# One-hot operands of a gate-matrix product: pairs of tokens interleaved, eight tokens written by each VectorE instruction

## The chip, the cores and the metric

The kernel runs on one core of a Trainium2 chip. The metric is the device time of one execution in microseconds (us). The kernel before took a median of 3380.77 us over three runs (3378.14 to 3381.57).

## The reference

The whole program is two transformer-like blocks over 512 tokens of 1024 features. The change lies in the last part of the second block, a feed-forward layer that gathers single-neuron experts by product keys:

```python
def peer_ffn(xn, w_q, sub_keys, u, v):
    def block(xb):
        q = (xb @ w_q).reshape(PEER_BLOCK, PEER_HEADS, 2, PEER_HALF)
        s = jnp.einsum('thpd,hpnd->thpn', q, sub_keys).astype(jnp.float32)
        s_top, i_top = lax.top_k(s, PEER_TOPK)
        cand = s_top[:, :, 0, :, None] + s_top[:, :, 1, None, :]
        cand_idx = i_top[:, :, 0, :, None] * PEER_N_KEYS + i_top[:, :, 1, None, :]
        ...
        best, pos = lax.top_k(cand, PEER_TOPK)
        expert = jnp.take_along_axis(cand_idx, pos, axis=-1)
        g = jax.nn.softmax(best, axis=-1)
        act = jax.nn.gelu(jnp.einsum('td,thkd->thk', xb, u[expert]), approximate=False)
        return jnp.einsum('thk,thkd->td', (g * act).astype(xb.dtype), v[expert])
```

There are 8 heads, 128 keys on each of the two sides, so 128 x 128 = 16384 experts, and each head of each token takes 16 of them. A token thus has 128 picks: two key numbers (k1 and k2) and a weight g for each.

## The kernel before, in words

**Dense experts.** For the last 128 tokens the kernel gathers the picked rows of u and v by indirect DMA. For the first 384 tokens (three tiles of 128, NDENSE is 3) it computes all 16384 experts: for each of 128 pieces of 128 experts, hidden = gelu(u piece x tokens) (u_task), then hidden times gates (weigh), then the product with the v piece (v_task, L1755). The gates are zero for experts that a token did not pick.

**The gate matrix.** For each token gate_matrix(i) makes the 128 x 128 matrix of gates G[k2, k1] as a product over the token's 128 picks: a one-hot of k2 (picks on the partitions, 128 keys along the row) as weights, and the weighted one-hot of k1 as the moving operand. Both are fp16; the weight is split into two fp16 parts, so a token takes two matmuls that add up in PSUM (L1443). `picks[i]` holds, per pick (partition) and token, k1, k2 and the two parts of the weight; `it16` holds the 128 key numbers in each partition. The steps of gate_matrix, four tokens at a time, are

- `rows` and `fill` (L1430 to L1437): three tiles for eight tokens each, of ten such tiles in all (tag "t", NT = 10). VectorE writes them with three narrow instructions of 128 elements per token: the one-hot of k2 (L1433), and for each part of the weight the one-hot of k1 times the part, in one instruction with two operations (L1436). The picks of the token are its per-partition scalars.
- `product` (L1443), two steps (eight tokens) later: eight matmuls of four tokens into one PSUM tile. PSUM has four such tiles in this phase, which the expert products of u_task use too.
- `store` (L1452, L1456), three steps (twelve tokens) later: ScalarE moves the PSUM tile in two halves to staging tiles; every sixteen tokens these go to DRAM (`gate_d`). `load_gates` (L1684) brings the gates of eight pieces back, and `weigh` (L1728) multiplies them into the hidden values.

```python
for t0 in range(0, 128 + 12, 4):
    if t0 - 12 in ps:
        store(t0 - 12, ps.pop(t0 - 12))
    ...
    if 0 <= t0 - 8 < 128:
        ps[t0 - 8] = product(t0 - 8, oh[(t0 - 8) // 8 * 8])
    yield
```

**The order of the work.** gate_matrix is a generator in a list of background work (`W.later`), one for each of the three token tiles, behind top-k steps of VectorE (`top_k`, L1314 to L1390) that find the picks. It runs between the first 28 products of u_task, which read the weights directly in fp32: 8 matmul instructions of 384 columns per piece at L1708, two records each in the trace, 16 records per piece. After each piece the pace of this stage (PACE[6] = 6.5) lets six or seven background steps follow. What is left over after the 28 pieces is run at once (`W.flush`), then the gates are loaded and the v products begin (L1755). Each engine works through its instructions in program order, in the order in which a scheduler has put them; VectorE's and ScalarE's order in this stage also holds the splitting of v pieces into two parts (L151 on VectorE, L143 on ScalarE, into tiles "hi" and "lo").

Other lines named below: L1378 is a VectorE comparison of top-k, 1024 fp16 elements, with an operand that is broadcast; L973 subtracts from each block of a cumulated sum one of its elements, repeated; L498 is a fp32 product of the first block with 128 columns; L883 is a projection of the second block; L1720 is the Gelu behind L1708.

Of the kernel before, what the change touches and what calls it, by code (L numbers as in the profile page):

```python
# [9 lines left out]
F16 = mybir.dt.float16  # L10
# [3 lines left out]
OP = mybir.AluOpType  # L14
# [155 lines left out]
def tile_kernel(ctx: ExitStack, tc: tile.TileContext, ins, out):  # L170
    nc = tc.nc
# [14 lines left out]
    def ps_tile(role="a"):  # L186
        tag, n = psum["roles"].get(role, psum["roles"]["a"])
        return psum["pool"].tile([128, 512], F32, tag=tag, bufs=n, name="ps")
# [101 lines left out]
    sm = ctx.enter_context(tc.tile_pool(name="sm", bufs=2))  # L290
    hp = ctx.enter_context(tc.tile_pool(name="hold", bufs=1))
    blocks = ExitStack()
    g = blocks.enter_context(tc.tile_pool(name="g", bufs=1, reuse_waits="tile"))
    NT = 10
# [5 lines left out]
    def tb(name, n=T + 2):  # L300
        return sm.tile([128, n], F32, tag="t", bufs=NT, name=name)
# [521 lines left out]
    it128 = hp.tile([128, 128], F32, name="it128")  # L823
# [2 lines left out]
    glp = hp.tile([128, 2, KD, 16], F32R, name="glp")  # L826
    idx = {NDENSE: hp.tile([128, NSLOT], I32, name="idx")}
    gw = {NDENSE: hp.tile([128, NSLOT], F32, name="gw")}
    it16 = hp.tile([128, 128], F16, name="it16")
    it1 = hp.tile([128, TOPK], F16, name="it1")  # L830
    picks = {i: hp.tile([128, 4, 128], F16, name=f"picks{i}") for i in range(NDENSE)}
    dram = ctx.enter_context(tc.tile_pool(name="dram", bufs=1, space=bass.MemoryType.DRAM))
# [4 lines left out]
    def second_block():  # L837
# [3 lines left out]
            def tables():  # L841
                for t, name in ((cols2, "cols2"), (it128, "it128"), (reset, "reset"), (wup, "wup")):
                    nc.sync.dma_start(t, ins[name])
                nc.vector.tensor_copy(it1, it128[:, :TOPK])
                nc.vector.tensor_copy(it16, it128)
                w = tb("glw", KD * 16).rearrange("p (k c) -> p k c", c=16)
                nc.sync.dma_start(w, ins["glw"])
                split_act([glp[:, 0], glp[:, 1]], w)
                for i in range(2):
                    m = g.tile([128, T], F32, tag="table", bufs=2, name="masks")[:, :512]  # L850
                    m = m.rearrange("p (a b) -> p a b", b=128)
                    nc.sync.dma_start(m, ins["masks"][:, 4 * i:4 * i + 4])
                    masks.extend(m[:, j] for j in range(4))

                l0, l1 = cols2[:, E_LG:E_LG + 4], cols2[:, E_LG + 4:E_LG + 8]
                mx, e0, e1 = (sm.tile([128, 4], F32, name=n) for n in ("mx", "e0", "e1"))
                nc.vector.tensor_tensor(out=mx, in0=l0, in1=l1, op=OP.max)
                nc.vector.tensor_tensor(out=e0, in0=l0, in1=mx, op=OP.subtract)
                nc.vector.tensor_tensor(out=e1, in0=l1, in1=mx, op=OP.subtract)
                nc.scalar.activation(e0, e0, AF.Exp)  # L860
                nc.scalar.activation(e1, e1, AF.Exp)
                nc.vector.tensor_tensor(out=e1, in0=e0, in1=e1, op=OP.add)
                nc.vector.reciprocal(out=e1, in_=e1)
                nc.vector.tensor_tensor(out=lb, in0=e0, in1=e1, op=OP.mult)
                nc.vector.tensor_scalar(out=omlb, in0=lb, scalar1=-1.0, scalar2=1.0, op0=OP.mult, op1=OP.add)
# [555 lines left out]
            def gate_matrix(i):  # L1421

                k1, k2, *w = (picks[i][:, j] for j in range(4))
                stage = []

                def rows(t0):

                    oh = [sm.tile([128, 8, 128], F16, tag="t", bufs=NT, name="oh") for _ in range(3)]
                    return oh

                def fill(t0, oh):
                    for t in range(t0, t0 + 4):
                        nc.vector.tensor_scalar(out=oh[0][:, t % 8], in0=it16, scalar1=k2[:, t:t + 1],  # L1433
                                                scalar2=None, op0=OP.is_equal)
                        for x, y in zip(oh[1:], w):
                            nc.vector.tensor_scalar(out=x[:, t % 8], in0=it16, scalar1=k1[:, t:t + 1],  # L1436
                                                    scalar2=y[:, t:t + 1], op0=OP.is_equal, op1=OP.mult)  # L1437

                def product(t0, oh):
                    ps = ps_tile("g").rearrange("p (t n) -> p t n", n=128)  # L1440
                    for t in range(4):
                        for j in (1, 2):
                            nc.tensor.matmul(ps[:, t], oh[0][:, t0 % 8 + t], oh[j][:, t0 % 8 + t],  # L1443
                                             start=j == 1, stop=j == 2)
                    return ps

# [8 lines left out]
                        if t0 % 16 == 12:  # L1455
                            nc.scalar.dma_start(gate_d[:, (128 * i + t0) // 16, j * 1024:(j + 1) * 1024], stage[j])  # L1456

                oh, ps = {}, {}
                for t0 in range(0, 128 + 12, 4):
                    if t0 - 12 in ps:  # L1460
                        store(t0 - 12, ps.pop(t0 - 12))
                    if t0 < 128:
                        if t0 % 8 == 0:
                            oh[t0] = rows(t0)
                        fill(t0, oh[t0 // 8 * 8])
                    if 0 <= t0 - 8 < 128:
                        ps[t0 - 8] = product(t0 - 8, oh[(t0 - 8) // 8 * 8])
                    yield
# [73 lines left out]
            for word in PLAN.split():  # L1542
# [4 lines left out]
                else:  # L1547
                    name = word.rstrip("01234")
# [402 lines left out]
```

## Time and profile before

| what | value |
|---|---|
| median of three runs | 3380.77 us (3378.14 to 3381.57) |
| profiled execution, its own time | 3379.18 us |
| span of the profiled execution | 3377.2 us |
| mean granted TensorE clock | 0.985 |
| TensorE busy | 98% of the span |
| VectorE busy | 64% |
| ScalarE busy | 39% |
| GpSimd busy | 5% |

The profile is one execution. Its span runs from the first to the last instruction; 1.98 us of the execution's time lie around it. The page cuts the span into 40 slices of 84.4 us; a digit is the busy share in tenths, and the row PEclk is the clock that TensorE was granted. Records whose operands have shape 128x384 or 128x512 with "f32" are fp32 products, those with "f16" the gate products.

### The profile page before, as it was taken

The page shows a single profiled execution, that of the slowest core. Times are in us where ns is not written, and L with a number is a line of the kernel's source. Part 1 is how long each engine was busy: PE and PEld are TensorE (multiplying, and loading weights), DVE is VectorE, ACT ScalarE, POOL GpSimd, SP SyncE. Part 2 cuts the span into 40 slices and gives each one's busy share as a digit, 9 for nine tenths or more (in the row PEclk, how much of TensorE's full clock was granted, in tenths as well). Part 3 has the DMA queues.
Part 4 walks back from the last instruction along what each step waited for, and adds up shares of the span by engine and source line. Part 5 has one row for each costly group of instructions (what it writes and reads, how often), then busy time and mean ns, then how long its engine had stood idle before and what let it go on. Part 6 is the DMA issues. An engine that isn't in the chain of part 4 may idle for free.

```text
span 3377.2 us, 52075 instructions
## 1 busy us (share of the span) xinstructions
PE 3313.5 (98%) x21063; PEld 2989.4 (89%) x21063; DVE 2152.3 (64%) x4979; ACT 1302.9 (39%) x2388; POOL 184.7 (5%) x132
## 2 busy tenths in 40 slices
PE   8999999999999999999999999898899999999999
PEld 7999999999899999999999988554589999999998
DVE  6545554334654555433566679999988888888544
ACT  5433333324433333332554543444433333333333
POOL 0000000000000000000000000000032222222000
PEclk9999999999999999999999999988999999999999
DMA  5222222223422222222422133334599998999542
GB/s 210 85 85 85 76 76 88 92 97 113 159 85 73 97 83 87 88 100 88 150 76 88 63 124 139 134 141 149 197 351 351 340 347 320 342 346 344 189 150 94
DMA packets 129968, 532.10 MB, mean 158 GB/s; under 512 B 9136, under 2 KB 60992, under 8 KB 73280
## 3 DMA queue, kind: packets, MB, share of 16 engines
q1 hardware_dynamic: 103520, 368.19, 30.6%
q0 software_dynamic: 18432, 134.23, 10.3%
q10 hardware_dynamic: 7776, 26.37, 2.0%
q8 instruction: 165, 2.70, 0.3%
q14 instruction: 75, 0.61, 0.1%
HBM read 501.48 MB, written 27.26 MB: 157 GB/s over the span
## 4 chain that ended last, share of the span: by engine, by line
PE 84%; DVE 12%; DMA 2%; ACT 1%; issue 1%; POOL 0%; DVEq 0%; ACTq 0%; POOLq 0%
PE ps L386 36%; PE ps L1755 13%; PE ps L1711 12%; PE ps L454 5%; DVE oh L1436 5%; PE ps L887 3%; DVE oh L1433 2%; PE ps L549 2%; PE ps L688 2%; PE ps L1004 2%; PE ps L1275 1%; PE ps L396 1%; PE ps L498 1%; PE ps L883 1%; PE ps L450 1%; DMA uv<-uv,idx 1%
## 5 line engine op out<-in xcount | busy, mean ns | idle before, releaser
L151 DVE TENSOR_TENSOR lo<-raw,hi 128x1024 fp32r<-128x1024 f32 x532 | 650.3, 1223 | 745.5 <-ACT hi L143 742.9
L143 ACT ACTIVATE hi<-raw 128x1024 fp32r<-128x1024 f32 x532 | 563.0, 1059 | 1390.4 <-PE ps L386 626.9
L386 PE MATMUL ps<-xnh,hi 128*128 128x256 f32 (+1 forms) x2464 | 513.7, 283 | 0.0
L386 PE MATMUL ps<-xnl,hi 128*128 128x256 f32 (+1 forms) x2464 | 513.5, 283 | 0.0
L386 PE MATMUL ps<-xnh,lo 128*128 128x256 f32 (+1 forms) x2464 | 512.8, 283 | 0.0
L1755 PE MATMUL ps<-hi,hw 128*128 128x512 f32 x1536 | 428.9, 395 | 10.3 <-DVE hw L204 9.3
L1711 PE MATMUL ps<-hn,hi 128*128 128x384 f32 x1600 | 408.4, 336 | 0.0
L386 PEld LDWEIGHTS ps<-xnh,lo 128*128 128x128 f32 x2464 | 385.8, 189 | 0.0
L386 PEld LDWEIGHTS ps<-xnh,hi 128*128 128x128 f32 x2464 | 384.7, 188 | 1.1
L386 PEld LDWEIGHTS ps<-xnl,hi 128*128 128x128 f32 x2464 | 384.4, 188 | 0.1
L1755 PEld LDWEIGHTS ps<-hi,hw 128*128 128x128 f32 x1536 | 288.2, 189 | 72.8 <-DVE hw L204 12.0
L1625 POOL DMA_INDIRECT uv<-uv,idx x128 | 184.5, 1441 | 2946.4 <-DVE hw L204 2450.5
L1711 PEld LDWEIGHTS ps<-hn,hi 128*128 128x128 f32 x1600 | 290.4, 188 | 4.3
L1711 PE MATMUL ps<-hn,lo 128*128 128x384 f32 x800 | 268.6, 336 | 0.0
L1755 PE MATMUL ps<-lo,hw 128*128 128x512 f32 x768 | 239.9, 392 | 0.0
L1436 DVE TENSOR_SCALAR oh<-it,picks 128x128 f16<-128x128 f16 x768 | 204.9, 313 | 0.0
L1708 PE MATMUL ps<-hn,raw 128*128 128x384 f32 x448 | 172.0, 545 | 1.8 <-ACT stage L1452 1.0
L1755 PEld LDWEIGHTS ps<-lo,hw 128*128 128x128 f32 x768 | 144.9, 189 | 32.0
L1653 DVE SCALAR_TENSOR_TENSOR acc<-uv,dots,acc 128x1024 f32<-128x1024 f32 x127 | 163.0, 1283 | 3.2
L1661 DVE SCALAR_TENSOR_TENSOR uv<-uv,hnT 128x1024 f32<-128x1024 f32 x128 | 155.7, 1218 | 10.8 <-DMA uv<-uv,idx 10.8
L1708 PEld LDWEIGHTS ps<-hn,raw 128*128 128x128 f32 x448 | 94.1, 215 | 67.1 <-issue 20.9
L1711 PEld LDWEIGHTS ps<-hn,lo 128*128 128x128 f32 x800 | 150.0, 188 | 0.1
(354 smaller groups left out, 5257.5 us busy)
## 6 DMA issues: line engine op xcount, KB each, us to landing
raw<-ws SPq DMA_DIRECT2D x313, 1024.0 KB, 4.8
gate_d<-stage ACTq DMA_DIRECT2D x48, 512.0 KB, 3.5
gates<-gate_d SPq DMA_DIRECT2D x16, 1536.0 KB, 9.7
dm<-decay_m SPq DMA_DIRECT2D x8, 264.0 KB, 5.7
vb<-vbias SPq DMA_DIRECT2D x8, 256.0 KB, 5.5
dc<-decay SPq DMA_DIRECT2D x8, 256.0 KB, 5.6
uv<-uv,idx POOLq DMA_INDIRECT x128, 8.3
h<-ht SPq DMA_DIRECT2D x2, 544.0 KB, 5.6
```

What stands on the lines that cost most here:

```text
L143: nc.scalar.activation(hi, raw[i], AF.Copy)
L151: nc.vector.tensor_tensor(out=lo, in0=r, in1=parts[i][0].bitcast(F32), op=OP.subtract)
L386: nc.tensor.matmul(t[:, :b - a], w[wi][:, off + k, :], x[k].t[xi][:, a:b], start=(k == 0 and n == 0), stop=(k == K - 1 and n == 2))
L454: nc.tensor.matmul(p, xn[k].t[xi][:, m0:m0 + mn], w[wi][:, kk, :], start=(k == 0 and n == 0), stop=(k == KD - 1 and n == 2))
L887: nc.tensor.matmul(p, parts[wi][:, k, :], x[k][:, xi], start=(k == 0 and n == 0), stop=(k == K - 1 and n == 2))
L1436: nc.vector.tensor_scalar(out=x[:, t % 8], in0=it16, scalar1=k1[:, t:t + 1], scalar2=y[:, t:t + 1], op0=OP.is_equal, op1=OP.mult)
L1625: nc.gpsimd.indirect_dma_start(out=t, out_offset=None, in_=ins["uv"], in_offset=bass.IndirectOffsetOnAxis(ap=idx[i][:, j:j + 1], axis=0))
L1653: nc.vector.scalar_tensor_tensor(out=acc, in0=v, scalar=dots[:, j:j + 1], in1=acc, op0=OP.mult, op1=OP.add)
L1661: nc.vector.scalar_tensor_tensor(out=u, in0=u, scalar=1.0, in1=hnT, op0=OP.mult, op1=OP.mult, accum_out=dots[:, j:j + 1])
L1708: nc.tensor.matmul(ps, w[0][:, k, :], tl["hn32"][k][:, :ND], start=k == 0, stop=k == KD - 1)
L1711: nc.tensor.matmul(ps, w[wi][:, k, :], tl["hn"][k][:, xi], start=(k == 0 and n == 0), stop=(k == KD - 1 and n == 2))
L1755: mm = nc.tensor.matmul(tl["acc"][t][b], h[:, hi, t * 128:(t + 1) * 128], w[vi][:, b * 512:(b + 1) * 512], start=(e == 0 and n == 0), stop ...
```

## The change

`it16` now holds each key number twice, side by side. A one-hot tile is still 128 x 1024 fp16 and still for eight tokens, but its layout is [4 pairs of tokens, 128 keys, 2 tokens of the pair]. For eight tokens VectorE writes two tiles with one instruction each, the bare one-hots of k1 and k2 (L1438 of the changed kernel, `rows`): the first operand is the key table, read again for each pair, the second are the picks of eight tokens, of which a pair is read again for each of the 128 keys. One step of four tokens later `weighed` multiplies the one-hot of k1 by each part of the weight into two more tiles (L1445). So a group of eight tokens takes four tiles instead of three, of the same ten, and 192 wide instructions take the place of 1152 narrow ones. The matmuls (now L1453) read a token's operands with a step of two elements. `store` is the same; lines behind gate_matrix move by 10 (L1452 to L1462, L1708 to L1718, L1720 to L1730, L1728 to L1738, L1755 to L1765).

```diff
--- before.py
+++ after.py
@@ -826,7 +826,7 @@
     glp = hp.tile([128, 2, KD, 16], F32R, name="glp")
     idx = {NDENSE: hp.tile([128, NSLOT], I32, name="idx")}
     gw = {NDENSE: hp.tile([128, NSLOT], F32, name="gw")}
-    it16 = hp.tile([128, 128], F16, name="it16")
+    it16 = hp.tile([128, 128, 2], F16, name="it16")
     it1 = hp.tile([128, TOPK], F16, name="it1")
     picks = {i: hp.tile([128, 4, 128], F16, name=f"picks{i}") for i in range(NDENSE)}
     dram = ctx.enter_context(tc.tile_pool(name="dram", bufs=1, space=bass.MemoryType.DRAM))
@@ -842,7 +842,7 @@
                 for t, name in ((cols2, "cols2"), (it128, "it128"), (reset, "reset"), (wup, "wup")):
                     nc.sync.dma_start(t, ins[name])
                 nc.vector.tensor_copy(it1, it128[:, :TOPK])
-                nc.vector.tensor_copy(it16, it128)
+                nc.vector.tensor_copy(it16, it128[:, :, None].to_broadcast([128, 128, 2]))
                 w = tb("glw", KD * 16).rearrange("p (k c) -> p k c", c=16)
                 nc.sync.dma_start(w, ins["glw"])
                 split_act([glp[:, 0], glp[:, 1]], w)
@@ -1421,26 +1421,36 @@
             def gate_matrix(i):
 
                 k1, k2, *w = (picks[i][:, j] for j in range(4))
+                full = [128, 4, 128, 2]
+                keys = it16[:, None].to_broadcast(full)
                 stage = []
 
+                def wide(x, t0):
+                    return x[:, t0:t0 + 8].rearrange("p (a b) -> p a b", b=2)[:, :, None, :].to_broadcast(full)
+
+                def row():
+                    return sm.tile([128, 4, 128, 2], F16, tag="t", bufs=NT, name="oh")
+
                 def rows(t0):
 
-                    oh = [sm.tile([128, 8, 128], F16, tag="t", bufs=NT, name="oh") for _ in range(3)]
+                    oh = [row() for _ in range(2)]
+                    for x, k in zip(oh, (k1, k2)):
+                        nc.vector.tensor_tensor(out=x, in0=keys, in1=wide(k, t0), op=OP.is_equal)
                     return oh
 
-                def fill(t0, oh):
-                    for t in range(t0, t0 + 4):
-                        nc.vector.tensor_scalar(out=oh[0][:, t % 8], in0=it16, scalar1=k2[:, t:t + 1],
-                                                scalar2=None, op0=OP.is_equal)
-                        for x, y in zip(oh[1:], w):
-                            nc.vector.tensor_scalar(out=x[:, t % 8], in0=it16, scalar1=k1[:, t:t + 1],
-                                                    scalar2=y[:, t:t + 1], op0=OP.is_equal, op1=OP.mult)
+                def weighed(t0, oh):
+
+                    parts = [row() for _ in w]
+                    for x, y in zip(parts, w):
+                        nc.vector.tensor_tensor(out=x, in0=oh[0], in1=wide(y, t0), op=OP.mult)
+                    return [oh[1], *parts]
 
                 def product(t0, oh):
                     ps = ps_tile("g").rearrange("p (t n) -> p t n", n=128)
                     for t in range(4):
+                        a, b = divmod(t0 % 8 + t, 2)
                         for j in (1, 2):
-                            nc.tensor.matmul(ps[:, t], oh[0][:, t0 % 8 + t], oh[j][:, t0 % 8 + t],
+                            nc.tensor.matmul(ps[:, t], oh[0][:, a, :, b], oh[j][:, a, :, b],
                                              start=j == 1, stop=j == 2)
                     return ps
 
@@ -1455,14 +1465,14 @@
                         if t0 % 16 == 12:
                             nc.scalar.dma_start(gate_d[:, (128 * i + t0) // 16, j * 1024:(j + 1) * 1024], stage[j])
 
-                oh, ps = {}, {}
+                raw, oh, ps = {}, {}, {}
                 for t0 in range(0, 128 + 12, 4):
                     if t0 - 12 in ps:
                         store(t0 - 12, ps.pop(t0 - 12))
-                    if t0 < 128:
-                        if t0 % 8 == 0:
-                            oh[t0] = rows(t0)
-                        fill(t0, oh[t0 // 8 * 8])
+                    if t0 % 8 == 0 and t0 < 128:
+                        raw[t0] = rows(t0)
+                    if t0 - 4 in raw:
+                        oh[t0 - 4] = weighed(t0 - 4, raw.pop(t0 - 4))
                     if 0 <= t0 - 8 < 128:
                         ps[t0 - 8] = product(t0 - 8, oh[(t0 - 8) // 8 * 8])
                     yield
```

On VectorE, in the gate matrix of the third token tile (picks2), the order before has for each token three rows; here the last token of a group of eight and the first of the next (oh_23599 and oh_23657 are their one-hots of k2):

```order
L1433 TENSOR_SCALAR oh_23599<-it16_100,picks2_104 128x128
L1436 TENSOR_SCALAR oh_23600<-it16_100,picks2_104 128x128
L1436 TENSOR_SCALAR oh_23601<-it16_100,picks2_104 128x128
L1433 TENSOR_SCALAR oh_23657<-it16_100,picks2_104 128x128
L1436 TENSOR_SCALAR oh_23658<-it16_100,picks2_104 128x128
L1436 TENSOR_SCALAR oh_23659<-it16_100,picks2_104 128x128
```

In the same place of the changed kernel two groups of eight tokens are eight rows:

```order
L1438 TENSOR_TENSOR oh_22592<-it16_100,picks2_104 128x1024
L1438 TENSOR_TENSOR oh_22593<-it16_100,picks2_104 128x1024
L1445 TENSOR_TENSOR oh_22609<-oh_22592,picks2_104 128x1024
L1445 TENSOR_TENSOR oh_22610<-oh_22592,picks2_104 128x1024
L1438 TENSOR_TENSOR oh_22626<-it16_100,picks2_104 128x1024
L1438 TENSOR_TENSOR oh_22627<-it16_100,picks2_104 128x1024
L1445 TENSOR_TENSOR oh_22645<-oh_22626,picks2_104 128x1024
L1445 TENSOR_TENSOR oh_22646<-oh_22626,picks2_104 128x1024
```

Twenty-four rows of 128 elements per group have become four of 1024, and nothing else stands between them here.

On TensorE, at the end of the gate products, the order before has the last gate products, 22 fp32 products of u_task (44 records), and the first v products (raw and hn32 are the u piece and the tokens, hw the weighted hidden values):

```order
L1443 MATMUL ps_23939<-oh_23875,oh_23873 128x128
L1708 MATMUL ps_23964<-hn32_20263,raw_22989 128x384 x2
L1708 MATMUL ps_23964<-hn32_20268,raw_22989 128x384 x4
L1708 MATMUL ps_23980<-hn32_20263,raw_23269 128x384 x4
L1708 MATMUL ps_23980<-hn32_20268,raw_23269 128x384 x4
L1708 MATMUL ps_23994<-hn32_20263,raw_23269 128x384 x4
L1708 MATMUL ps_23994<-hn32_20268,raw_23269 128x384 x4
L1755 MATMUL ps_24020<-hi_23976,hw_24017 128x512
```

The changed kernel has there

```order
L1453 MATMUL ps_23027<-oh_22998,oh_22981 128x128
L1718 MATMUL ps_23038<-hn32_20263,raw_22400 128x384 x4
L1718 MATMUL ps_23038<-hn32_20268,raw_22400 128x384 x4
L1718 MATMUL ps_23052<-hn32_20263,raw_22400 128x384 x4
L1718 MATMUL ps_23052<-hn32_20268,raw_22400 128x384 x4
L1718 MATMUL ps_23068<-hn32_20263,raw_22585 128x384 x4
L1718 MATMUL ps_23068<-hn32_20268,raw_22585 128x384 x4
L1718 MATMUL ps_23082<-hn32_20263,raw_22585 128x384 x4
L1718 MATMUL ps_23082<-hn32_20268,raw_22585 128x384 x4
L1765 MATMUL ps_23108<-hi_23064,hw_23105 128x512
```

Between the last gate product and the first v product stand 32 fp32 products (64 records) instead of 22.

## Rows read from the trace of the kernel before

**Rows 1.** The page, parts 1 and 2: engine shares, granted clock by slice.

```profile
PE 3313.5 (98%) x21063; PEld 2989.4 (89%) x21063; DVE 2152.3 (64%) x4979; ACT 1302.9 (39%) x2388; POOL 184.7 (5%) x132
...
PEclk9999999999999999999999999988999999999999
```

**Rows 2.** Windows: stretch, length, busy PE, PEld, DVE, ACT, POOL, PEclk, DMA, GB/s.

```profile
2050.00:2100.00 50.00, 50.00 (x256) 44.65 (x255) 49.84 (x298) 16.83 (x48) 0.00 (x0) 1.00 0.35 127
2250.00:2300.00 50.00, 44.16 (x214) 23.75 (x214) 50.00 (x248) 20.69 (x45) 0.00 (x0) 0.80 0.39 149
2114.77:2401.20 286.43, 257.37 (x1214) 146.39 (x1213) 284.28 (x1462) 118.95 (x258) 0.00 (x0) 0.86 0.40 145
```

**Rows 3.** Timeline of VectorE: start, us from first to last, what, how many.

```profile
2114.17 0.68 DVE L1378 TENSOR_TENSOR eq<-eq,it 128x1024 f16<-128x1024 f16 x1
2114.77 0.57 DVE L1433 TENSOR_SCALAR oh<-it,picks 128x128 f16<-128x128 f16 x3
...
2124.27 0.25 DVE L1433 TENSOR_SCALAR oh<-it,picks 128x128 f16<-128x128 f16 x1
...
2126.09 0.25 DVE L1433 TENSOR_SCALAR oh<-it,picks 128x128 f16<-128x128 f16 x1
...
2378.19 1.22 DVE L151 TENSOR_TENSOR lo<-raw,hi 128x1024 fp32r<-128x1024 f32 x1
2379.32 0.54 DVE L1436 TENSOR_SCALAR oh<-it,picks 128x128 f16<-128x128 f16 x2
...
2380.54 0.54 DVE L1436 TENSOR_SCALAR oh<-it,picks 128x128 f16<-128x128 f16 x2
```

**Rows 4.** Timeline of TensorE's matmuls, in brackets the idle time before them.

```profile
2124.27 23.39 PE L1708 MATMUL ps<-hn,raw 128*128 128x384 f32 x72
2147.49 1.06 PE L1443 MATMUL ps<-oh 128*128 128x128 f16 x16
...
2313.61 6.70 PE L1708 MATMUL ps<-hn,raw 128*128 128x384 f32 x16
2320.15 1.71 PE L1443 MATMUL ps<-oh 128*128 128x128 f16 x27
2322.03 0.44 PE L1443 MATMUL ps<-oh 128*128 128x128 f16 x2 [0.17 <-DVE oh L1436]
2322.64 0.44 PE L1443 MATMUL ps<-oh 128*128 128x128 f16 x2 [0.17 <-DVE oh L1436]
...
2386.19 0.50 PE L1443 MATMUL ps<-oh 128*128 128x128 f16 x6
2386.53 14.41 PE L1708 MATMUL ps<-hn,raw 128*128 128x384 f32 x44
...
2401.20 0.74 PE L1755 MATMUL ps<-hi,hw 128*128 128x512 f32 x2 [0.27 <-ACT hw L203]
```

**Rows 5.** Groups of VectorE by shape: busy us, mean ns, idle before.

```profile
L973 DVE TENSOR_TENSOR e<-cum 128x512 f32<-128x512 f32 x4 | 2.5, 684 | 0.0
```

**Rows 6.** Timeline of TensorE near 1251 us (L498) and 2601 us (L1755).

```profile
1250.89 0.28 PE L498 MATMUL ps<-ql,kh 128*128 128x128 f32 x1
1251.01 0.28 PE L498 MATMUL ps<-qh,kl 128*128 128x128 f32 x1
...
2601.08 1.08 PE L1755 MATMUL ps<-hi,hw 128*128 128x512 f32 x4
2601.99 0.62 PE L1755 MATMUL ps<-lo,hw 128*128 128x512 f32 x2
```

**Rows 7.** Groups of weight loads by shape, 2100 to 2400 us.

```profile
L1443 PEld LDWEIGHTS <-oh 128*128 128x128 f16 x768 | 54.1, 98 | 72.5 <-DVE oh L1433 26.2 <-DVE oh L1436 25.5 <-issue 4.7
L883 PEld LDWEIGHTS ps<-hn,raw 128*128 128x128 f32 x41 | 7.6, 190 | 0.9
```

**Rows 8.** Waits of TensorE: who for whom, us in all, how many, longest.

```profile
PE ps L1443 <- ACT stage L1452: 5.3, 5, 3.0
```

**Rows 9.** Timeline of ScalarE: evictions of gate products.

```profile
2172.93 3.63 ACT L1452 ACTIVATE stage<-ps 128x256 f32<-128x256 f32 x8
```

**Rows 10.** Windows as in rows 2, L1708 alone: PE, PEld, PEclk, DMA, GB/s.

```profile
2114.77:2401.20 286.43, 167.84 (x436) 91.51 (x434) 0.86 0.40 145
```

## The prediction

> **What bounds the kernel now.** I read the page's engine shares and slices first, then the windows of the stage that the change touches, then the timelines of VectorE and TensorE inside it. Over the whole span TensorE is busy 98% of the time, so a change to VectorE's work looks worthless; the reader is to see that this average hides one stage. In slices 26 to 29 the granted clock drops to 0.8 and 0.9 [rows 1]. The windows show why: just ahead of the stage TensorE is busy without a gap at a granted clock of 1.00, and in the middle of it VectorE is busy 50.00 us of each 50 while TensorE is busy 44 at a granted clock of 0.80 [rows 2], a mean over its two levels, 1.2 and 2.4 GHz.
>
> The timeline of VectorE says what it is busy with. The first one-hot starts at 2114.77 and the last at 2380.54, and tokens follow each other at (2126.09 - 2124.27)/3 = 0.607 us: one L1433 and two L1436 [rows 3]. 384 tokens make 233.0 us of the 266.3 us from the first start to the end of the last; the other 33.3 us are top-k steps and three weight splits. On TensorE the same stage reads as a beat: 16 records of the expert products (L1708) in 6.70 us, then 27 gate products that lie ready, and then pairs of gate products (one token each) that start 0.61 us apart, each after an idle 0.17 us that ends with L1436 [rows 4]. So TensorE waits for one-hots, token by token, and the clock falls on top of it. The stage ends for TensorE where the first L1755 starts, at 2401.20: 286.4 us after the first one-hot. That interval is what the change can shorten; I leave what comes before and behind it as it is.
>
> **What the change costs and saves, part by part.**
>
> *VectorE.* Removed: 1152 narrow operations, 233.0 us. Added: 48 groups of eight tokens with four wide operations each, 192 in all, two comparisons and two products. Their price is not in the trace as such. The lower bound is L1378, also a comparison of 1024 fp16 elements with an operand that is read again and again: it starts at 2114.17 and the next operation at 2114.77, so 0.60 us [rows 3]. The upper bound is a 1024-element operation on 4-byte data, L151: 2379.32 - 2378.19 = 1.13 us [rows 3]. The new thing is the operand that holds only two neighbouring elements and repeats them 128 times. I take 0.60, since type, size and kind of operation are those of L1378, and since repeating did not slow L973, which subtracts one repeated element from each block: 512 elements in 684 ns [rows 5], against 1.22 us for the 1024 of L151, a slope of 1.05 ns per element as for plain operands. Sum: 192 x 0.60 = 115.2 us, plus the other 33.3, makes 148 us where 266 stood. The wider key table adds half of a 128-element copy, once, early: nothing.
>
> *A rule against it.* The Trainium skill (Vector Engine (DVE) Microarchitecture Reference, 5.2 Measured stream behaviour on trn2) says that a port streams at full rate only in runs of at least two adjacent 4-byte words and lists 1.73 against 1.054 ns per column for one source that hops at each element; a pair of fp16 is one such word. By those figures the wide operation would take 0.60 x 1.73/1.054 = 0.98 us, an estimate, and the sum below would end near 3337. No run here shows it yet; it is the third rival.
>
> *TensorE's own work.* Once VectorE is ahead, TensorE's queue sets the stage. Between 2114.77 and 2401.20 it holds 436 records of L1708 at (2147.49 - 2124.27)/72 = 0.322 us, 140.4 us; 768 gate products at 0.056 us (16 in a row take 1.06 us and 6 take 0.50, so ten take 0.56), 43.0 us [rows 4]; and 13 small transposes and key products, about 1.5 us. That is 185 us. The change makes both operands of the gate products step over every second element, 4 bytes from column to column. Lower bound: nothing. Upper bound: 0.12 us, the distance of two 128-column matmuls on 4-byte operands in L498 [rows 6]. For the moving side I take nothing, since L1755 streams 512 columns of 4 bytes in (2601.99 - 2601.08)/4 = 0.228 us, 0.057 per 128 [rows 6]. For the weights it is less clear: a weight load of L1443 takes 98 ns and one of 4-byte weights 190 [rows 7], and which of the two a stepped fp16 load resembles no row says. I take the 98, as the data type is that of the row, and keep 0.12 for the range. The Trainium skill (TensorE: Matmul & The Clock Gate, Weight-path perf modes) has the fast load take 128 weights that are not FP32, packed or strided; by it the sum stays as it is.
>
> *What TensorE still waits for.* First, the beginning: in the first gate products TensorE waits 5.3 us in five waits for PSUM tiles that ScalarE has not emptied, because ScalarE stands behind VectorE's top-k steps there [rows 8]. Those steps stay: 5 us. Second, and next in line once one-hots come early: after each expert product TensorE has 6 to 7 batches of four tokens in a row, at 8 x 0.056 = 0.45 us each, while ScalarE needs two evictions of 3.63/8 = 0.45 us [rows 9] per batch, 0.90 us. Four PSUM tiles serve both, one of them the expert product's. The fourth to sixth batch and the next expert product each wait for the eviction three batches back; the fourth eviction ends at 0.45 + 4 x 0.90 = 4.05 us, where six batches alone would take 2.7, so 1.35 us per run, and 96 batches in runs of 6.5 make some 15 of them: 20 us. ScalarE in total, 192 x 0.45 = 87 us and a few Gelus, is not a bound. Third, VectorE's lead: a group now takes four tiles of the ten instead of three, so it can be about two groups ahead; a run eats 3.25 groups in some 4 us, in which VectorE adds 1.7. Just enough: nothing. Fourth, the end: in the trace 15.0 us pass from the last gate products (2386.19) to L1755, for eviction, store, load of the gates and weighting; 44 records of L1708 cover it now, and 64 stand there in the new order, 20.6 us [rows 4]. Covered.
>
> *Weights.* 436 records are 27 expert pieces; they are wanted every 210/27 = 7.8 us instead of every 10.6. The DMA engines are 40% busy in the stage [rows 2], so there is room.
>
> *Sum.* 185 + 5 + 20 = 210 us where 286.4 stood: 76 us less. VectorE's 148 us plus the 20.1 us from its last one-hot to L1755 stay below that. The profiled execution took 3379.18 us (a span of 3377.2 and 1.98 around it); 3379.2 - 76 = 3303, and the median of the runs lies 1.6 us higher: **3305 us**.
>
> **The rivals.**
>
> *TensorE slows on stepped operands* (0.12 us per gate product). For it: no row has a stepped fp16 weight load. Against it: L1755's columns. Then the product work is 768 x 0.12 = 92 us, TensorE's queue 234 us, and evictions keep up (0.96 us per batch against 0.90), so only the 5 us remain: 239 us, 47 us less, 3334.
>
> *The clock stays low.* The many short PSUM waits might keep the granted clock at the stage's present mean of 0.86 [rows 2]. L1708 is now busy longer by 27 us than 436 x 0.322 would be (167.8 us [rows 10]); if that stays, 3332.
>
> *VectorE does not get two elements per cycle.* If the repeated pair costs the packing, the wide operation takes from 0.9 us, half as long again as L1378, to the upper bound of 1.13. VectorE then needs 33.3 + 192 x 0.9 = 206 us and the 20.1 behind it, 226 in all, 3321 at least, and at 1.13 us 250 + 20.1 = 270, 3364. Against it stand L1378 and L973.
>
> *Slower than before.* The same place and one more step: repeated reads of one word that serialise. It decides from (266.3 - 33.3)/192 = 1.21 us per wide operation on; at 1.30 us VectorE needs 283 us and the stage 303, 17 us more than now, 3397. No row points there: L151, with three 4-byte operands, lies below it at 1.13. That the change does nothing at all would need just that 1.21 us.
>
> **How the numbers follow.** Forecast 0.70 (its own range 3290 to 3318, from half the PSUM waits to some clock loss); stepped operands 0.12; clock 0.05; no packing 0.09; slower 0.04. The range reaches over the forecast, the stepped operands and the clock, 0.87, less their edges: 3288 to 3338. About 0.2%, 7 us, is what a measurement tells from no change. Faster by more: 0.70 + 0.12 + 0.05 and most of no packing, 0.94; within it 0.02; slower 0.04.
>
> **What would show it.** Right: L1438 and L1445 at about 0.68 us mean, VectorE no longer full in the stage and idle before L1438 because of TensorE; the waits of L1453 on one-hots almost gone, with ScalarE's evictions as its new releaser; a granted clock near 1.0; the interval from the first one-hot to the first L1765 near 210 us. Wrong: wide operations at 1 us or more, gate products at 0.1 us apart, or L1765 waiting long for the gates because the last store came late.

## The result, and the profile after

| | before | after |
|---|---|---|
| median | 3379.82 us (3378.14 to 3381.57, 4 runs) | 3293.15 us (3289.29 to 3295.42, 4 runs) |
| ratio, 95% interval | | 0.9742 (0.9725 to 0.9759) |
| span of the profiled execution | 3377.2 us | 3291.6 us |

The change takes 86.7 us off, 10.7 more than the 76 forecast, so the time is 12 below the 3305 and inside the range. Here are the page's shares and granted clock of the changed kernel, and its windows for the interval that the forecast is about, from the first one-hot to the first v product (columns as in rows 2; the second row counts the expert products at L1718 alone):

```profile
PE 3250.3 (99%) x21063; PEld 2974.2 (90%) x21063; DVE 2036.7 (62%) x4019; ACT 1302.2 (40%) x2388; POOL 186.3 (6%) x132
...
PEclk9999999999999999999999999999999999999999
```

```profile
2115.82:2326.21 210.39, 195.10 (x1217) 129.46 (x1215) 182.47 (x555) 123.86 (x270) 0.00 (x0) 1.00 0.55 205
...
2115.82:2326.21 210.39, 146.39 (x439) 81.40 (x437) 1.00 0.55 205
```

The dip of the clock in slices 26 to 29 [rows 1] is gone. The interval takes 210.4 us instead of 286.4 [rows 2], 76.0 less, with VectorE busy 182 of it instead of 284. The granted clock is 1.00 instead of 0.86, and L1718 is busy 146 us instead of 168 [rows 10]. Ahead of the interval 1.0 us was lost; behind the first v product the span is 965.4 us long instead of 976.0. So 76.0 + 10.6 - 1.0 make the 85.6 us between the spans. VectorE's groups of one-hots, and its timeline late in the stage:

```profile
L1438 DVE TENSOR_TENSOR oh<-it,picks 128x1024 f16<-128x1024 f16 x96 | 63.0, 686 | 22.4 <-PE ps L1453 22.1
L1445 DVE TENSOR_TENSOR oh<-oh,picks 128x1024 f16<-128x1024 f16 x96 | 61.9, 684 | 0.0
```

```profile
2288.42 0.69 DVE L1438 TENSOR_TENSOR oh<-it,picks 128x1024 f16<-128x1024 f16 x1 [2.21 <-PE ps L1453]
2289.03 1.29 DVE L1445 TENSOR_TENSOR oh<-oh,picks 128x1024 f16<-128x1024 f16 x2
2290.23 1.29 DVE L1438 TENSOR_TENSOR oh<-it,picks 128x1024 f16<-128x1024 f16 x2
2291.43 1.29 DVE L1445 TENSOR_TENSOR oh<-oh,picks 128x1024 f16<-128x1024 f16 x2
...
2298.31 1.29 DVE L1445 TENSOR_TENSOR oh<-oh,picks 128x1024 f16<-128x1024 f16 x2
```

Two wide operations start 1.20 us after the two before: 0.60 us each. VectorE now waits for TensorE, 22 us in all, and TensorE waits less than 2 us for one-hots. On TensorE the timeline shows what the stage has become (compare [rows 4]), and the table of its waits in the interval (who for whom, us, times, longest) sums it:

```profile
2176.63 2.42 PE L1453 MATMUL ps<-oh 128*128 128x128 f16 x39
2179.27 0.63 PE L1453 MATMUL ps<-oh 128*128 128x128 f16 x8 [0.22 <-ACT stage L1462]
2180.16 0.63 PE L1453 MATMUL ps<-oh 128*128 128x128 f16 x8 [0.26 <-DVE oh L1438]
2181.06 0.63 PE L1453 MATMUL ps<-oh 128*128 128x128 f16 x8 [0.27 <-ACT stage L1462]
2181.95 5.43 PE L1718 MATMUL ps<-hn,raw 128*128 128x384 f32 x16 [0.26 <-ACT stage L1462]
2187.22 2.49 PE L1453 MATMUL ps<-oh 128*128 128x128 f16 x40
...
2302.47 20.91 PE L1718 MATMUL ps<-hn,raw 128*128 128x384 f32 x64 [0.27 <-ACT stage L1462]
2326.21 1.21 PE L1765 MATMUL ps<-hi,hw 128*128 128x512 f32 x2 [2.84 <-ACT hid L1730]
```

```profile
PE ps L1453 <- ACT stage L1462: 5.6, 17, 1.1
PE ps L1718 <- ACT stage L1462: 4.7, 12, 0.7
...
PE ps L1453 <- DVE oh L1438: 1.5, 6, 0.3
...
PE ps L1453 <- DVE oh L1445: 0.3, 1, 0.3
```

A run of gate products starts at full pace, (2.49 - 0.63)/32 = 0.058 us each, and then falls to one batch of eight per 0.90 us, the time of ScalarE's two evictions [rows 9]. Of such a 0.90 us the products are 0.47 and the idle time shown is 0.26; the other 0.17 is what a row of eight lasts beyond 8 x 0.058 (0.63 - 0.47), the drain of its last product, which the table does not count.

The 2.84 us ahead of the first v product are a wait of their own. ScalarE's timeline there:

```profile
2317.11 0.99 ACT L203 ACTIVATE hw<-hid 128x384 fp32r<-128x384 f32 x2 [2.16 <-DVE hid L1738]
...
2325.26 0.52 ACT L203 ACTIVATE hn<-hn 128x384 fp32r<-128x384 f32 x1 [3.26 <-DVE hn L1595]
2325.69 0.47 ACT L1730 ACTIVATE hid<-ps 128x384 f32<-128x384 f32 x1
```

The weighted values of the first two pieces are written long before, the first parts by 2318.1 and the second parts (L204, on VectorE) by 2321.5. What ends 0.05 us before the first v product starts is the Gelu that empties the last expert product's PSUM tile; the kernel divides PSUM anew for the v products. In ScalarE's order this Gelu stands behind an operation that waits 3.26 us for VectorE.

### The profile page after: what moved, and what is told of

Its sections match the earlier page's. It is cut to its first block, busy times and chain, and to the rows that moved or that the text cites. A ratio compares the mean times of both kernels' runs of the same rounds, so it can differ in the third digit from the quotient of the medians.

```text
span 3291.6 us, 51099 instructions
## 1 busy us (share of the span) xinstructions
PE 3250.3 (99%) x21063; PEld 2974.2 (90%) x21063; DVE 2036.7 (62%) x4019; ACT 1302.2 (40%) x2388; POOL 186.3 (6%) x132
## 3 DMA queue, kind: packets, MB, share of 16 engines
q0 software_dynamic: 18432, 134.23, 10.6%
## 5 line engine op out<-in xcount | busy, mean ns | idle before, releaser
L151 DVE TENSOR_TENSOR lo<-raw,hi 128x1024 fp32r<-128x1024 f32 x532 | 650.6, 1224 | 753.3 <-ACT hi L143 748.4
L1765 PE MATMUL ps<-hi,hw 128*128 128x512 f32 x1536 | 427.0, 393 | 3.3 <-ACT hid L1730 2.8
L1765 PEld LDWEIGHTS ps<-hi,hw 128*128 128x128 f32 x1536 | 287.7, 188 | 63.6 <-ACT hid L1730 3.5
L1765 PE MATMUL ps<-lo,hw 128*128 128x512 f32 x768 | 239.5, 392 | 0.0
L1765 PEld LDWEIGHTS ps<-lo,hw 128*128 128x128 f32 x768 | 144.7, 188 | 32.1
L1718 PE MATMUL ps<-hn,raw 128*128 128x384 f32 x448 | 149.5, 490 | 5.0 <-ACT stage L1462 4.7
L887 PE MATMUL ps<-x,hi 128*128 128x256 f32 x768 | 141.4, 288 | 4.0 <-ACT x L274 3.4
L1718 PEld LDWEIGHTS ps<-hn,raw 128*128 128x128 f32 x448 | 83.4, 190 | 62.6 <-ACT stage L1462 8.1
```

The costliest lines, as they stand in the source:

```text
L151: nc.vector.tensor_tensor(out=lo, in0=r, in1=parts[i][0].bitcast(F32), op=OP.subtract)
L887: nc.tensor.matmul(p, parts[wi][:, k, :], x[k][:, xi], start=(k == 0 and n == 0), stop=(k == K - 1 and n == 2))
L1718: nc.tensor.matmul(ps, w[0][:, k, :], tl["hn32"][k][:, :ND], start=k == 0, stop=k == KD - 1)
L1765: mm = nc.tensor.matmul(tl["acc"][t][b], h[:, hi, t * 128:(t + 1) * 128], w[vi][:, b * 512:(b + 1) * 512], start=(e == 0 and n == 0), stop ...
```

## Experiments

Two theories were put to the chip. Mine: VectorE's 1152 short operations set the stage, the wide ones cost 0.60 us because of the pairs, and what is left is TensorE's own queue and ScalarE's evictions. Against it: the step of TensorE's operands, or the ring of tiles, or ScalarE in total sets the new time. Times are medians; the kernel before ran beside each at 3379 to 3381 us.

**The changed kernel again**, as a yardstick.

> The changed kernel itself, once more, as the yardstick of the other runs on this chip. Expected: within 0.2% of 3293 us, the first one-hot to the first v product 210 us apart, wide operations 0.60 us apart, granted clock 1.00 in that stretch.

Measured: 3291.02 us, ratio 0.9735 (0.972 to 0.975), interval 211.0 us, behind it 963.6 us. So the yardstick is 3291 to 3293 us.

**Without the pairs.** The tiles and the key table change their shape accordingly, and the matmuls read a token's 128 elements in a row:

```diff
-                full = [128, 4, 128, 2]
+                full = [128, 8, 128]
...
-                    return x[:, t0:t0 + 8].rearrange("p (a b) -> p a b", b=2)[:, :, None, :].to_broadcast(full)
+                    return x[:, t0:t0 + 8][:, :, None].to_broadcast(full)
```

> Same wide operations, but without the pairs: a tile is 8 tokens x 128 keys, the picks operand repeats one fp16 element 128 times, and the matmuls read 128 elements in a row. Theory (the pair is what keeps two elements per cycle): one repeated element loses it, an operation takes 1.07 to 1.2 us, VectorE needs 33 + 192 x 1.1 = 245 us and 20 behind it, 265 instead of 210, and the 10 us of waits behind the stage come back: 3345 to 3370 us. Rival (repeating does no harm, as for L973 and L1378): 0.60 us and the time of the changed kernel, within 5 us.

Measured: 3373.58 us, ratio 0.9977 (0.9968 to 0.9986). VectorE's timeline and the window of the interval:

```profile
2201.26 2.37 DVE L1445 TENSOR_TENSOR oh<-oh,picks 128x1024 f16<-128x1024 f16 x2
2203.53 2.37 DVE L1438 TENSOR_TENSOR oh<-it,picks 128x1024 f16<-128x1024 f16 x2
...
2116.30:2400.84 284.54, 223.32 (x1216) 142.05 (x1214) 280.09 (x551) 122.32 (x270) 0.00 (x0) 0.87 0.39 147
```

The same 192 wide operations, only with one 2-byte element repeated in place of two, take 2.27/2 = 1.135 us each, VectorE is full again, the granted clock is back at 0.87, and 8 us remain of the 87. Of these 8 the interval has only 1.9 (284.5 against 286.4); the rest lies behind the first v product, where the span is 969.0 us long instead of 976.0. In this form, fewer instructions alone bring almost nothing in the stage; the pair brings the gain. The Trainium skill (Vector Engine (DVE) Microarchitecture Reference, 5.1 Performance modes — why throughput varies by op and dtype) says just that: two 16-bit results per cycle need every operand to advance by one element in its innermost dimension, and a two-source operation that read one element again and again ran at one per cycle. By the runs here the two cases differ by 0.53 us per 1024 elements. The interval is 284.5 us where I expected 265: the operations take 218 us instead of 211, VectorE's other work 42 instead of 33 (below), and 24 us instead of 20 lie behind the last one-hot. The time is 4 us above the expected range. Behind the first v product 7.1 us of waits for split hidden values are back.

**TensorE without the step.** Each gate product reads 128 elements in a row:

```diff
-                        a, b = divmod(t0 % 8 + t, 2)
+                        a = t0 % 8 + t
...
-                            nc.tensor.matmul(ps[:, t], oh[0][:, a, :, b], oh[j][:, a, :, b],
+                            nc.tensor.matmul(ps[:, t], *(x.rearrange("p a k b -> p (a k b)")[:, 128 * a:128 * a + 128] for x in (oh[0], oh[j])),
```

> The changed kernel, only each gate product reads 128 elements in a row of the interleaved tile, so the operands of two tokens are mixed: the separation of the two tokens of a pair is left out. Every engine's order is the same, so the only difference is the step of TensorE's operands. Theory (the step costs TensorE nothing): gate products 0.058 us apart as now, the time within 3 us of the changed kernel. Rival (stepped weights or columns cost): 0.056 us or less and a stage shorter by 1.5 us for each 2 ns per product.

Measured: 3291.96 us, ratio 0.9739 (0.9724 to 0.9754), interval 210.1 us. The same two rows as above, in this kernel:

```profile
2181.36 0.61 PE L1453 MATMUL ps<-oh 128*128 128x128 f16 x8 [0.28 <-ACT stage L1462]
...
2187.52 2.43 PE L1453 MATMUL ps<-oh 128*128 128x128 f16 x40
```

(2.43 - 0.61)/32 = 0.057 us in this row. Over the whole stage, two gate products with no wait between them start 56 ns apart (the median) where the changed kernel has 58. So the step has a price, as the rival had it: 2 ns per product, 1.5 us over the 768. It does not reach the time, since the waits for ScalarE grow from 10.3 to 11.9 us.

**Expert and gate products interleaved.** An order-only edge makes each eighth of an expert product follow the gate products issued before it:

```diff
+                            W.last = nc.tensor.matmul(ps[:, t], oh[0][:, a, :, b], oh[j][:, a, :, b],
...
+                        mm = nc.tensor.matmul(ps, w[0][:, k, :], tl["hn32"][k][:, :ND], start=k == 0, stop=k == KD - 1)
+                        if W.last:
+                            edge(W.last, mm)
+                            W.last = None
```

> The changed kernel with one more order on TensorE: the expert product's next eighth waits for the gate products issued before it, so that 8 or 16 gate products stand between each 4 records of expert products instead of 32 to 56 in one run. Theory (what is left in the stage is that a run of gate products fills the four PSUM tiles faster than ScalarE empties them; 29 such waits, 10.3 us idle and some 0.16 us of drain each, 15 us): these waits go, about 50 more changes between the two kinds of products cost 0.1 us each, so 8 to 12 us less: 3280 to 3286 us, stage 199 to 203 us. Rival (ScalarE's total or VectorE is the limit): no change, or TensorE waits for one-hots in place of PSUM tiles.

Measured: 3283.56 us (3279.39 to 3287.31), ratio 0.9707 (0.9694 to 0.972); none of its five runs is as slow as any of the changed kernel's. TensorE's timeline, and the window of the interval:

```profile
2161.08 1.09 PE L1454 MATMUL ps<-oh 128*128 128x128 f16 x16
2162.01 1.50 PE L1719 MATMUL ps<-hn,raw 128*128 128x384 f32 x4
2163.35 1.10 PE L1454 MATMUL ps<-oh 128*128 128x128 f16 x16
...
2116.35:2311.42 195.07, 190.52 (x1216) 126.13 (x1215) 183.81 (x556) 128.28 (x269) 0.00 (x0) 1.00 0.59 215
```

Four records take 1.34 us until the next gate product, 0.05 more than 4 x 0.322, half of what I had put for a change. The other way, from a gate product to an expert product, it is 0.058 us, as between two gate products. The waits for PSUM tiles fall from 10.3 to 0.3 us and the interval from 210.4 to 195.1: ScalarE had time enough, only the runs were too long for four tiles. Of these 15 us some 8 reach the time: in this execution, the slowest of the five, the part behind is 974.1 us, 9 to 10 longer than in the two profiles above, 3.2 of it a wait for split hidden values (0.2 to 0.4 there); for the rest TensorE is busy longer (964.2 us against 958.3). This is the fastest version of the study.

**More work for VectorE**: each product by a part of the weight is written twice.

```diff
+                        for _ in range(2):
+                            nc.vector.tensor_tensor(out=x, in0=oh[0], in1=wide(y, t0), op=OP.mult)
```

> The changed kernel with each product by a part of the weight written twice (the second time the same values), so 96 wide operations more. Theory (VectorE's queue is the next bound at its price of 0.605 us): it needs 33 + 288 x 0.605 = 207 us and 20 behind its last one-hot, the stage 225 to 232 us instead of 210, waits for one-hots come back and those for PSUM tiles fall; being full, VectorE also carries top-k work behind the stage, and the first v products wait some 8 us for it again: 3308 to 3322 us. Rival (the stage is set by ScalarE and PSUM, VectorE's 22 idle us hide the work): below 3300.

Measured: 3339.06 us, ratio 0.9872 (0.9857 to 0.9887). The interval is 250.6 us, and TensorE waits for one-hots again:

```profile
PE ps L1454 <- DVE oh L1446: 21.4, 14, 2.2
```

The mechanism holds (VectorE is the next bound), the size does not (3308 to 3322 was expected): from the first one-hot (2114.74) to the end of the last (2341.4) VectorE needs 227 us, of which 288 x 0.60 = 173 are wide operations, 8 are waits for TensorE and some 45 are other work, not 33; and 24 us, not 20, lie behind. The granted clock, 0.93 in this interval, falls again as well.

**Eight tiles in the ring**, `NT = 8` instead of 10.

> The changed kernel with eight one-hot tiles of the ring instead of ten, so VectorE can be two groups ahead instead of two and a half. Theory (the lead is just enough, since VectorE makes a group in 2.4 us and a run eats one in 1.8): waits for one-hots rise from 2 to at most 6 us, the time by 0 to 5 us. Rival (the ring is what holds the stage, as VectorE's 22 us of waiting for TensorE would let one think): over 10 us slower.

Measured: 3308.17 us, ratio 0.9787 (0.9772 to 0.9802): 15 us slower than the changed kernel, the rival's side. VectorE's and TensorE's waits in the interval of 225.1 us:

```profile
DVE oh L1445 <- PE ps L1453: 36.7, 14, 5.4
...
PE ps L1453 <- ACT stage L1462: 10.5, 18, 0.7
PE ps L1718 <- ACT stage L1462: 6.3, 6, 1.6
PE ps L1765 <- ACT hw L203: 5.1, 1, 5.1
PE ps L1453 <- DVE oh L1445: 4.1, 9, 0.5
```

TensorE's waits for PSUM tiles and for one-hots grew, and at the end it now waits 5.1 us for weighted values (L203), since 48 records instead of 64 stand there to cover the gates. So the lead depends on the ring: two tiles fewer cost 15 us where I expected 5 at most. With ten tiles TensorE waits 1.8 us for one-hots; nine, or more than ten, were not tried.

**VectorE moves out half of each PSUM tile.**

```diff
-                        nc.scalar.activation(
...
+                        if j:
+                            nc.vector.tensor_scalar(out=out, in0=ps[:, :, 64:], scalar1=1.0 / WSCALE, scalar2=None,
+                                                    op0=OP.mult)
```

> The changed kernel with the second half of each PSUM tile moved out by VectorE instead of ScalarE. Theory (runs of gate products wait for two evictions of 0.45 us in a row on ScalarE): at 0.45 us per batch on each of two engines the waits for PSUM tiles fall from 10.3 to 3 us or less, while VectorE's 96 evictions of some 0.35 us take the place of its 22 idle us and of some 12 more: 3284 to 3294 us. Rival (VectorE's evictions stand behind wide operations of 0.6 us each): the waits only change their releaser, 3295 us or more.

Measured: 3326.53 us, ratio 0.9841 (0.9828 to 0.9855): the rival. Its waits in the interval of 238.7 us:

```profile
PE ps L1453 <- DVE stage L1464: 23.9, 32, 1.1
PE ps L1721 <- DVE stage L1464: 9.3, 9, 2.6
```

The waits tripled and changed their releaser, as the rival says. But VectorE's total grew too: its evictions start 0.43 us apart, not the 0.35 I had put, which makes 41 us for the 96, and it is busy 220 us of the 239. How much comes from evictions that stand behind 0.6 us operations and how much from this longer queue, the run does not separate. Behind the first v product 12.7 us of waits for split hidden values are back, and the part behind is 976.0 us long.

**The 10 us behind the stage.** Before, the first v products wait for the split of weighted hidden values, and the granted clock is 0.93 in the first 50 us; after, these waits are 0.4 us in all and the clock is 0.97. The windows of the 50 us behind the first v product, before and after, and the waits of TensorE from there to the end of the span:

```profile
2401.20:2451.20 50.00, 42.07 (x168) 32.91 (x169) 43.79 (x105) 20.20 (x34) 0.28 (x1) 0.93 0.66 209
...
PE ps L1755 <- DVE hw L204: 9.3, 5, 4.1
PE ps L1755 <- ACT hw L203: 0.9, 2, 0.7
```

```profile
2326.20:2376.20 50.00, 49.56 (x211) 40.12 (x212) 40.66 (x69) 18.92 (x31) 9.31 (x5) 0.97 0.90 316
...
PE ps L1765 <- ACT hid L1730: 2.8, 1, 2.8
PE ps L1765 <- DVE hw L204: 0.4, 1, 0.4
```

(The 2.8 us stand ahead of the first v product and belong to the interval.) In the first 100 us VectorE spends some 12 us on top-k of the last 128 tokens before and 2 after, so this was my first suspect; the order of multiplications and splits was the second. Three edits of the kernel before and two of the interleaved kernel:

```diff
-PACE = (3, 1, 2, 2, 2, 3.75, 6.5, 1.5, 1, 0.7)
+PACE = (3, 1, 2, 2, 2, 3.75, 6.5, 0.5, 1, 0.7)
...
-GAT = 6
+GAT = 18
```

> The kernel before, only with the top-k steps of the last 128 tokens let in three times less often behind the stage and not forced through before the eighteenth v piece instead of the sixth. The stage itself stays as it was (286 us). Theory (the other 10 us of the gain came from VectorE having this top-k work left over when the v products begin; with VectorE full, 9 us of waits for weighted hidden values): those waits fall from 9.3 to about 4 us, 4 to 6 us less: about 3375. Rival (the waits come from the gates' transfer and splitting, not from top-k): no change, within 2 us.

Measured: 3380.11 us, ratio 0.9994 (0.9985 to 1.0003); the waits for split hidden values are 8.1 us. No change; but the edit did not do what it was meant to. In the first 100 us behind the first v product VectorE spends 16.6 us on top-k here, against 11.9 before. So this run says nothing about top-k.

```diff
+            if e > 1:
+                edge(tl["sub"], mul)
```

> The kernel before, only with VectorE's order at the v products pinned: the multiplication of a piece's hidden values with its gates comes right behind the split of the piece before, instead of eight multiplications in a row whenever gates land. The stage stays at 286 us. Theory (the first v products wait 9.3 us for split hidden values because those splits stand behind rows of multiplications): the waits fall below 4 us, 5 to 8 us less: about 3374. Rival (the waits come from the sheer amount of VectorE's work there, top-k included): the waits stay at 8 us or more, the time within 3 us of before.

Measured: 3383.68 us, ratio 1.001 (1.0001 to 1.0019):

```profile
PE ps L1758 <- ACT hw L1736: 6.5, 1, 6.5
PE ps L1758 <- DVE hw L1737: 6.3, 3, 3.3
```

The waits grew to 12.8 us, and the part behind the first v product to 984.0.

```diff
-                                experts.late.append(top_k(2 * s + t, b, x))
+                                W.later(top_k(2 * s + t, b, x), name="top")
```

> The kernel before, only with all top-k steps of the last 128 tokens put ahead of the one-hots instead of behind them. Theory (what is carried behind the stage is top-k work of a full VectorE): the waits for split hidden values behind the stage fall from 9.3 to below 2 us, the part behind the first v product from 976 to some 966 us, and the stage or what is ahead of it grows by the 12 to 25 us of that work, since VectorE is full: 3380 to 3396 us. Rival (order of multiplications and splits): the waits stay near 8 us and the time grows by the full work.

Measured: 3397.38 us, ratio 1.0051 (1.0036 to 1.0067):

```profile
PE ps L1755 <- ACT hw L203: 11.1, 1, 11.1
PE ps L1755 <- DVE hw L204: 9.3, 3, 6.5
```

The 11.1 us stand ahead of the first v product, which starts 20 us later than before. Behind it no top-k is left, and the 9.3 us stay; the part behind is 971.6 us long, not the 966 expected. The kernel without the pairs says the same: 1.0 us of top-k in the first 100 us, and 7.1 us of waits. With the first of these edits, and with the second, in the interleaved kernel:

> The kernel with interleaved expert and gate products, with the top-k steps of the last 128 tokens let in less often behind the stage as well. Theory: its two waits for weighted hidden values behind the stage (3.2 us) fall below 1 us: 2 to 3 us less than the 3283.6 of the interleaved kernel. Rival (they are not top-k's): the same time.

> The kernel with interleaved expert and gate products, and with VectorE's order at the v products pinned as in the pinned kernel before. Theory: its stage stays at 195 to 198 us, and the 3 to 8 us of waits for split hidden values behind it fall below 2: 3277 to 3282 us. Rival: no change from the 3283.6 of the interleaved kernel.

Measured: 3287.05 us (ratio 0.9722, 0.9708 to 0.9735) for the first and 3287.68 us (ratio 0.9726, 0.9713 to 0.9739) for the second; waits of 8.0 and 6.4 us. Neither is better than the interleaved kernel; the first had little to take away, as only 1.4 us of top-k stand in those 100 us of the interleaved kernel (2.8 with the edit). So the amount of top-k work is not the cause. Of the order of multiplications and splits one other was tried, and it is no better, which does not clear the order as it was. The arrival of the gates, for which VectorE's multiplications wait too (3.7 us in the kernel before from 2386 to 2450), was not varied. That the waits fell to 0.4 us or less is seen in three profiles with the changed order (after, its repeat, and the one without the step). With the same changes and eight tiles they are 3.3 us, interleaved 3.2, and where VectorE has more to do in the stage they are back: 4.8 us with products written twice, 7.1 without the pairs, 12.7 with VectorE's evictions. Why they fell stays open.

## Why the prediction was right, and where it was not

- **What bounds the kernel: right.** VectorE's short operations held the stage, and the average of 64% hid it. The interval that the forecast named went from 286.4 to 210.4 us; it said 210.
- **The price of a wide operation: right**, 0.60 us, but one reason for it was not. That L973 repeats an element at no cost says nothing here: its 512 elements of 4 bytes take 0.60 us from start to start, as long as 1024 of 2 bytes in L1378, so it had no such rate to lose. Without the pair the price is 1.135 us, the upper bound taken from L151. The rule of the Trainium skill that I weighed against the row (Vector Engine (DVE) Microarchitecture Reference, 5.2 Measured stream behaviour on trn2) would have given 0.98 us and 3337 us; the trace, with 0.60 us, does not agree. The row decided rightly, and it was the rule of section 5.1, named above, that bore on the case.
- **VectorE's total: the term "plus the other 33.3" was mis-sized.** After, it is some 45 us: 2299.6 - 2115.8 = 183.8, less 192 x 0.60 and 23 of waits. What grew is top-k: some 30 us of it stood between the first and the last one-hot before, 43 after, and of its 12 us in the first 100 us behind the first v product 2 are left. That is the order of the changed kernel, not VectorE's free time: without the pairs VectorE is full, and it is 42 us too. (The 33.3 also held two weight splits, not three.) Here it cost nothing, since VectorE had 23 us to spare; in the kernel with products written twice it is 12 of the 20 us that VectorE's queue lasts beyond the 207 expected.
- **TensorE's own work: right**, 439 x 0.322 + 768 x 0.058 + 1.5 = 187 us where I had 185. The rival of stepped operands (0.12 us) is out: the step costs 2 ns, where I had nothing.
- **PSUM waits: the right mechanism, too large.** I had 5 + 20 us; 29 waits show 10.3 us idle and, with 0.17 us of drain each, 15. The 5 us of the beginning did not stay as I had said: the waits of the first gate products, up to 3.0 us before [rows 8], are 0.7 us at most. The interleaved kernel, which takes them away, gave 15 back.
- **"Just enough: nothing" for the lead: nearly**, 1.8 us of idle time for one-hots. **"Covered" for the end: right for the gates**, but a term is missing, the 2.84 us that TensorE waits for the last Gelu to empty its PSUM tile. Own work, PSUM waits, one-hots (with the drain of these seven waits) and the Gelu make 187 + 15 + 3 + 3 = 208 of the 210.4. So the 210 was right with errors in it that cancel, and as a number it was partly luck.
- **The clock: right.** 1.00 in the stage; the rival in which short waits keep it low is out.
- **The step that failed: "I leave what comes before and behind it as it is".** Behind the first v product 10.6 us went, some 9.5 of it waits. This is most of the 12 us by which the time lies under the forecast. Its cause stays open; in the kernel without the pairs, where VectorE is as full as before, 7 of these us are gone too, so not all of it hangs on VectorE's free time.
- **The slower rival** needed 1.21 us per operation; even without the pair it is 1.135, and that kernel is still 0.2% faster than before.

## What to carry to other kernels

Where many short operations on 2-byte data can become a wide one, look at the innermost step of each operand first: here a repeated single element nearly halved the rate (1.135 against 0.60 us), interleaving two items so that a pair is repeated restored it, and the matmul that then steps over every second element paid 2 ns. When a busy engine is relieved, sum the next one's queue together with the buffers between them: here the remaining waits came in bursts, and an order that spreads the bursts was worth another 8 us. And do not hold the work behind the stage fixed in the forecast: list what waits there for the engine that gets free.

## What was not expected of the hardware

One repeated fp16 element in a two-operand operation of VectorE costs 0.53 us more per 1024 elements than a repeated pair (1.135 against 0.60 us). A stepped fp16 weight load is as fast as a contiguous one: L1453's take 97 ns with the step, 98 ns without, as before [rows 7]. Going from fp16 products to fp32 ones and back costs TensorE 0.05 us in the interleaved kernel.
